# The input norm of a hybrid decoder layer: weight spread over partitions in PSUM, factor and weight in one pass, buffers on the other side of SBUF, products of the identity first

## The chip, the cores and the metric

The kernel runs on one core of a Trainium2 chip. The metric is the device time of one execution in microseconds. Three runs of the kernel before gave 758.95, 758.96 and 759.19 us, median 758.96 us. Engines are named as the profile names them: PE (TensorE), DVE (VectorE), ACT (ScalarE), POOL (GpSimd), SP (the queue that issues most DMAs).

## The reference, cut to what matters

The program is one decoder layer on 512 tokens of width 1024. The change touches only its first step, the RMS norm that feeds the input projection:

```
def _rmsnorm(x, g):
    xf = x.astype(jnp.float32)
    y = xf * lax.rsqrt(jnp.mean(xf * xf, axis=-1, keepdims=True) + NORM_EPS)
    return y.astype(x.dtype) * g
...
    h = _rmsnorm(x, norm_g[i])
    proj = h @ w_in[i]
```

Everything after it (three token mixers, merge, output projection, per-layer embedding, final norm) is unchanged.

## The kernel before, in words

Products run on PE from split operands: a value v is kept as a high part (`hH`, `wh`) and a low part v - high (`hL`, `wl`), and each product is three: high x high, low x high, high x low (`mm` on line 61, called in `fm_block`). `h` is needed transposed, with its 1024 channels on the partitions in 8 blocks of 128 and the 512 tokens along the free side: `hH` and `hL`, 128 x 8 x 512.

The start of the program makes them (lines 198 to 226). x comes in as four tiles of 128 tokens (`xs_`). For each tile t, ACT squares it with a running sum (L213), DVE scales the sum (L214), POOL takes the power -1/2 (L215), which is the row factor `rsx`, and DVE multiplies the tile by it (L216). Then, for each half a of 512 channels, PE transposes four 128 x 128 blocks into PSUM (`xt_ps`, L221), DVE multiplies by the norm weight, which stands one value per partition by then (`ngp`, L223), ACT rounds the result to the high part (L224), and DVE or POOL subtracts for the low part (L225; table `XL`). The buffers of this stage (`xp`: `xs_`, `sqj`, `tg`) lie on SBUF's left side and are given back at `xp_ctx.close()`; the pools opened after it take their place, `cpp` among them, which holds `kc2`, `w1t` and `w2t`.

The first consumer is the block of the compression inputs (lines 249 to 264, "kc" below): for two halves of 256 tokens and two projections kv, 24 products each of 256 columns, 96 in all. It needs four loads of `w_in` (`wr`), rounded by ACT (`wh`, L77) and subtracted by DVE (`wl`, L78; the table `KL` names the engine). Each load covers four of the eight channel blocks, 12 products in each half. ACT copies the PSUM results into `kc2` (L263, L264); two PSUM buffers alternate (`pmm`). After it come the blocks of `rs_block`, 24 products of 512 columns each.

POOL makes the constants of the whole kernel before anything else (masks, indicators: lines 96 to 132, and `prow`, `hm`). Parameters come in as rows of `prow` (14 small DMAs on SP), and PE transposes them (`par_ps`, L268).

Each engine works off its instructions in order. The order is set by a scheduler at build time from its own estimates; the program can pin it (`tc.issue_after(x)` puts a block behind instruction x on x's engine, `tc.keep_in_program_order` keeps the order as written).

Of the kernel before, what the change touches and what calls it, by code (L numbers as in the profile page):

```python
# [17 lines left out]
NEG = -1e30  # L18
WE, NR, NH, NL = 560, 4, 5, 5
NG = 6  # L20
XL = "GV"
XB = 4
XP = 3
KL = "V"
KCA = 3
BS = 3
BO = 1
# [12 lines left out]
def f(ap):  # L40
    return ap.bitcast(F32)
# [3 lines left out]
def hybrid_kernel(ctx, tc, x, p, norm_g, w_in, cmp_w1, cmp_w2, cmp_pe, sg_ln_g, sg_ln_b, sg_w, sg_b,  # L45
# [49 lines left out]
    identb = const.tile([128, 128], BF, name="identb")
    V.tensor_copy(identb, ident)
    trib = const.tile([128, 128], BF, name="trib")
    G.memset(trib, 0.0)
    G.affine_select(out=trib, in_=trib, pattern=[[-1, 128]], compare_op=OP.is_ge, fill=NEG, base=0,
                    channel_multiplier=1)  # L100
    cmask = const.tile([128, 4, 32], BF, name="cmask")
    G.memset(cmask, 0.0)
    G.affine_select(out=cmask, in_=cmask, pattern=[[128, 4], [-16, 32]], compare_op=OP.is_ge, fill=NEG,
                    base=-31, channel_multiplier=1)
    rowm = const.tile([128, 1], F32, name="rowm")
    G.memset(rowm, 1.0)
    G.affine_select(out=rowm, in_=rowm, pattern=[[0, 1]], compare_op=OP.is_ge, fill=0.0, base=-31,
                    channel_multiplier=1)
    gmask = const.tile([128, 2, 64], BF, name="gmask")
    G.memset(gmask, 1.0)  # L110
    for r in (0, 64):
        for ar in range(2):
            G.affine_select(out=gmask[r:r + 64, ar, :], in_=gmask[r:r + 64, ar, :], pattern=[[1, 64]],
                            compare_op=OP.is_ge, fill=0.0, base=ar - 1, channel_multiplier=-1)
    smask = const.tile([128, 8, 64], BF, name="smask")
    G.memset(smask, 1.0)
    G.memset(smask[:, :, 0:1], 0.0)
    tri = const.tile([128, 128], BF, name="tri")
    G.memset(tri, 1.0)
    G.affine_select(out=tri, in_=tri, pattern=[[1, 128]], compare_op=OP.is_ge, fill=0.0, base=0,  # L120
                    channel_multiplier=-1)
    mhalf = const.tile([128, 32], F32, name="mhalf")
    G.memset(mhalf, -0.5)
    bones = const.tile([128, 128], BF, name="bones")
    G.memset(bones, 0.0)
    G.memset(bones[0:64, 0:64], 1.0)
    G.memset(bones[64:128, 64:128], 1.0)
    hind = const.tile([128, 4, 8], F32, name="hind")
    G.memset(hind, 0.0)
    for q in range(4):  # L130
        for e in range(2):
            G.memset(hind[e * 64:e * 64 + 64, q, 2 * q + e:2 * q + e + 1], 1.0)

    ng8 = const.tile([8, 128], F32, name="ng8")
    ngp = const.tile([128, 8], F32, name="ngp")
# [10 lines left out]
    hH = hp.tile([128, 8, 512], R, name="hH")  # L146
    hL = hp.tile([128, 8, 512], R, name="hL")
# [56 lines left out]
    dr = {}  # L204
    for nm, w in (("su", 512), ("sv", 512), ("sz", 512), ("rz", 512), ("nz", 512), ("y1", 512), ("sg", 512)):
        dr[nm] = tc.dram_tile([NG * 128 if nm == "sg" else 512, w], F32, name="dr_" + nm)
    ng_ps = xps.tile([128, 8], F32, tag="par", name="ng_ps", bufs=1)
    PE.transpose(ng_ps, ng8, ident[0:8, 0:8])
    V.tensor_copy(ngp, ng_ps)
    for t in range(4):  # L210
        ts = slice(t * 128, (t + 1) * 128)
        sqj = xp.tile([128, 1024], F32, tag="sqj", name="sqj", bufs=2)
        S.activation(sqj, xs_[:, t, :], AF.Square, accum_out=ssx[:, t:t + 1])  # L213
        V.tensor_scalar(rsx[:, t:t + 1], ssx[:, t:t + 1], 1.0 / 1024, 1e-6, op0=OP.mult, op1=OP.add)  # L214
        G.tensor_tensor(rsx[:, t:t + 1], rsx[:, t:t + 1], mhalf[:, 0:1], OP.pow)  # L215
# [90 lines left out]
    for kv in range(2):  # L306
# [10 lines left out]
        else:  # L317
            V.tensor_copy(sl, slp.rearrange("p (g n) -> p g n", g=2).unsqueeze(2).to_broadcast([128, 2, 4, 32]))
            for g in range(2):
# [4 lines left out]
                                       op0=OP.mult, op1=OP.subtract)  # L324
# [39 lines left out]
    for i, src in ((0, rk_w2), (1, rk_a2)):  # L364
        a, o = (slice(0, 64), slice(64, 128)) if i == 0 else (slice(64, 128), slice(0, 64))
# [39 lines left out]
    for q in range(4):  # L405
        rs_block(q)
        rs_block(8 + q)
        ps = rps.tile([128, 4, 128], F32, tag="y0", name="v_ps")
# [64 lines left out]
        for c0 in (0, 4):  # L473
            ps = rps.tile([128, 4, 128], F32, tag="y1", name="bk_ps")
# [63 lines left out]
    for c in range(8):  # L538
# [40 lines left out]
        if u == 1:  # L579
            t = c // 2  # L580
            ts = slice(t * 128, (t + 1) * 128)
# [16 lines left out]
            ps = rps.tile([128, 2, 2, 2, 64], F32, tag="g", name="yt_ps")  # L598
# [75 lines left out]
    for g in range(8):  # L674
# [3 lines left out]
                               op0=OP.add, op1=OP.mult)  # L678
# [318 lines left out]
```

## Time and profile before

| | |
|---|---|
| median of three runs | 758.96 us |
| profiled execution, its own time | 758.88 us |
| its span | 757.1 us |
| PE busy | 720.5 us (95%) |
| DVE, ACT, POOL busy | 403.1, 353.7, 327.6 us |
| first product of the kc block that uses `wl` | 17.44 us |
| first product of the block after it (512 columns) | 31.13 us |

Times in rows count from the span's start; 1.78 us of the execution's own time lie outside it. PE works through the program almost without a gap, so what counts for the change is at what time PE leaves the kc block.

### The profile page before, as it was taken

How to read it: one execution, taken by the hardware profiler on the slowest of the kernel's cores; microseconds unless marked ns; L12 is line 12 of the kernel's file. 1: busy time of each engine (PE TensorE's matmuls, PEld its weight loads, DVE VectorE, ACT ScalarE, POOL GpSimd, SP SyncE). 2: the span in 40 equal slices, each digit the busy share in tenths (PEclk: the TensorE clock that was granted, in tenths of full speed). 3: DMA queues.
4: the chain of work that ended last, by engine and by line, in shares of the span. 5: the costliest groups of instructions: out<-in, count | busy, mean ns of one | idle time of the engine just before them, and what ended most of it. 6: DMA issues, size and time to landing. Idle time of an engine off the chain costs nothing.

```text
span 757.1 us, 13075 instructions
## 1 busy us (share of the span) xinstructions
PE 720.5 (95%) x4941; PEld 610.3 (81%) x4941; DVE 403.1 (53%) x747; ACT 353.7 (47%) x743; POOL 327.6 (43%) x304
## 2 busy tenths in 40 slices
PE   4999999999996999999899999989999999999995
PEld 4888788899875987778777777867877888998995
DVE  6531688658817553456558456387655222216335
ACT  6454565533351332334464655476654333127453
POOL 6455731020335343424534335533445656256563
PEclk9999999999998999999999999999999999999999
DMA  5853222234553353346434222211117433222222
GB/s 197 186 142 85 64 73 59 72 97 118 147 171 111 100 165 112 103 140 182 138 84 125 57 56 56 71 29 42 43 47 250 121 98 110 72 98 75 79 70 112
DMA packets 106689, 78.73 MB, mean 104 GB/s; under 512 B 5569, under 2 KB 97282, under 8 KB 106626
## 3 DMA queue, kind: packets, MB, share of 16 engines
q1 hardware_dynamic: 105890, 75.27, 34.6%
q10 hardware_dynamic: 736, 2.63, 0.8%
q8 instruction: 39, 0.64, 0.3%
q14 instruction: 24, 0.20, 0.1%
HBM read 67.91 MB, written 9.96 MB: 103 GB/s over the span
## 4 chain that ended last, share of the span: by engine, by line
PE 83%; DVE 6%; DMA 3%; ACT 3%; issue 2%; POOL 1%; SPq 0%; ACTq 0%; POOLq 0%; DVEq 0%
PE mm_ps L61 66%; PE s_ps L61 3%; PE o_ps L61 2%; PE g_ps L61 2%; PE p_ps L861 2%; PE Yp L61 1%; DMA vn<-dr_sv 1%; DMA lnb<-in_sg_ln_b_dram 1%; PE r_ps L61 1%; DVE mx L847 1%; PE mx_ps L61 1%; DVE vn L671 1%; DVE pl L865 1%; ACT wh L77 1%; DMA zs<-dr_y 1%
## 5 line engine op out<-in xcount | busy, mean ns | idle before, releaser
L78 POOL TENSOR_TENSOR wl<-wr,wh 128x512 fp32r<-128x512 f32 (+1 forms) x168 | 225.0, 1348 | 292.8 <-ACT wh L77 279.1
L77 ACT CAST wh<-wr 128x512 fp32r<-128x512 f32 (+1 forms) x194 | 119.1, 620 | 162.7 <-PE mm_ps L61 112.3
L61 PE MATMUL mm_ps<-hH,wh 128*128 128x512 f32 (+1 forms) x440 | 174.9, 397 | 5.7 <-ACT gate L747 2.8
L61 PE MATMUL mm_ps<-hL,wh 128*128 128x512 f32 (+1 forms) x440 | 172.9, 393 | 0.0
L61 PE MATMUL mm_ps<-hH,wl 128*128 128x512 f32 (+1 forms) x440 | 172.2, 392 | 0.0
L61 PEld LDWEIGHTS mm_ps<-hH,wh 128*128 128x128 f32 x440 | 83.9, 191 | 24.0 <-ACT gate L747 3.5
L61 PEld LDWEIGHTS mm_ps<-hH,wl 128*128 128x128 f32 x440 | 83.8, 191 | 17.9 <-DVE wl L78 0.3
L61 PEld LDWEIGHTS mm_ps<-hL,wh 128*128 128x128 f32 x440 | 84.0, 191 | 16.7 <-issue 0.2
L61 PE MATMUL mm_ps<-wh,hL 128*128 128x256 f32 (+1 forms) x224 | 65.3, 292 | 0.0
L61 PE MATMUL mm_ps<-wl,hH 128*128 128x256 f32 (+1 forms) x224 | 64.7, 289 | 0.0
L61 PE MATMUL mm_ps<-wh,hH 128*128 128x256 f32 (+1 forms) x224 | 64.3, 289 | 0.0
L61 PEld LDWEIGHTS mm_ps<-wh,hH 128*128 128x128 f32 x224 | 42.8, 192 | 1.3 <-issue 0.5
L61 PEld LDWEIGHTS mm_ps<-wh,hL 128*128 128x128 f32 x224 | 43.0, 192 | 0.9 <-issue 0.5
L61 PEld LDWEIGHTS mm_ps<-wl,hH 128*128 128x128 f32 x224 | 42.9, 191 | 0.8
L865 DVE TENSOR_TENSOR pl<-p_ps,ph 128x512 fp32r<-128x512 f32 x40 | 27.1, 684 | 26.8 <-ACT ph L864 26.7
L61 PE MATMUL mm_ps<-ysH,wh 128*128 128x512 f32 x96 | 38.6, 402 | 0.2 <-ACT ysH L716 0.2
L61 PE MATMUL mm_ps<-ysL,wh 128*128 128x512 f32 x96 | 38.4, 400 | 0.2 <-DVE ysL L717 0.2
L61 PE MATMUL mm_ps<-ysH,wl 128*128 128x512 f32 x96 | 38.2, 398 | 0.0
L848 ACT ACTIVATE P<-s_ps,mx 128x512 f32<-128x512 f32 (+3 forms) x64 | 33.4, 532 | 7.8 <-DVE mx L847 5.5
L61 PE MATMUL mm_ps<-wh,mH 128*128 128x256 f32 x128 | 36.1, 286 | 0.6 <-DVE x L910 0.6
L61 PE MATMUL mm_ps<-wl,hT 128*128 128x256 f32 x128 | 35.8, 281 | 0.0
L61 PE MATMUL mm_ps<-wl,mH 128*128 128x256 f32 x128 | 35.8, 281 | 0.0
(336 smaller groups left out, 1437.1 us busy)
## 6 DMA issues: line engine op xcount, KB each, us to landing
wr<-in_w_in_dram SPq DMA_DIRECT2D x130, 256.0 KB
wr<-in_w_branch_dram SPq DMA_DIRECT2D x24, 256.0 KB
wr<-in_w_o_dram SPq DMA_DIRECT2D x16, 256.0 KB
wr<-in_w_ple_gate_dram SPq DMA_DIRECT2D x16, 256.0 KB
xs__129<-in_x_dram SPq DMA_DIRECT2D x4, 512.0 KB
w1t<-in_cmp_w_dram SPq DMA_DIRECT2D x4, 512.0 KB
x<-in_x_dram ACTq DMA_DIRECT2D x4, 512.0 KB
out_dram<-x SPq DMA_DIRECT2D x8, 256.0 KB
```

Of the source, the lines that this page charges most:

```text
L61: return PE.matmul(o, a, b, start=start, stop=stop, **kw).ins
L77: S.copy(h[:, :m], raw[:, :m])
L78: ph_["l"].tensor_tensor(l[:, :m], raw[:, :m], f(h[:, :m]), OP.subtract)
L671: V.tensor_scalar(vn[:, t, :], vn[:, t, :], mv[:, t, 0:1], rs4[:, t:t + 1], op0=OP.subtract, op1=OP.mult)
L847: V.tensor_reduce(mx[:, hh:hh + 1], s_ps[:, :W], axis=AX.X, op=OP.max, negate=True)
L848: S.activation(P[:, hh, :W], s_ps[:, :W], AF.Exp, bias=mx[:, hh:hh + 1], accum_out=sm[:, hh:hh + 1])
L861: PE.transpose(p_ps[:, hh * 128:hh * 128 + 128], P[:, hh, kt * 128:kt * 128 + 128], ident)
L865: V.tensor_tensor(pl, p_ps, f(ph), OP.subtract)
```

## The change

The norm weight is loaded as one row of 1024 (`ngr`) and spread over all partitions by two products with a column of ones, into two PSUM banks (`ngb`). DVE then applies row factor and weight at once to each half tile, before the transposes (`scalar_tensor_tensor`), so that the product with `ngp` after them (L223) goes, and ACT and DVE take high and low part straight from PSUM. The order of DVE's instructions is written out. 14 products of the identity with itself stand at the head of PE's program (`wu`). `XP` (PSUM buffers of the transposes) goes from 3 to 4. The four `wl` of the kc block, and all four low parts `hL` of POOL, change engine: `wl` to POOL (`KL`), `hL` to DVE. All constants but `ident`, `mhalf`, `one` and the zeros of `kc2` are made behind the fourth power on POOL (`issue_after(pws[3])`). The pools `xp` and `pw` lie on SBUF's right side.

```
-XL = "GV"
-XB = 4
-XP = 3
-KL = "V"
+XP = 4
+WU = 14
+KL = "G"
...
-    xp = xp_ctx.enter_context(tc.tile_pool(name="xp", bufs=1))
+    xp = xp_ctx.enter_context(tc.tile_pool(name="xp", bufs=1, side="right"))
...
-    S.dma_start(ng8, norm_g[0].rearrange("(a b) -> a b", b=128))
+    ngr = xp.tile([1, 1024], F32, name="ngr")
+    one = xp.tile([1, 128], F32, name="one")
+    S.dma_start(ngr, norm_g)
+    G.memset(one, 1.0)
...
-    ng_ps = xps.tile([128, 8], F32, tag="par", name="ng_ps", bufs=1)
-    PE.transpose(ng_ps, ng8, ident[0:8, 0:8])
-    V.tensor_copy(ngp, ng_ps)
+    wu = pmm.tile([128, 512], F32, tag="mm", name="wu")
+    for _ in range(WU):
+        mm(wu[:, 0:128], ident, ident, True, True)
+    ngb = xps.tile([128, 2, 512], F32, tag="ngb", name="ngb", bufs=1)
+    for a in range(2):
+        mm(ngb[:, a, :], one, ngr[:, a * 512:a * 512 + 512], True, True)
+    pin = tc.keep_in_program_order
...
-        V.tensor_scalar(xs_[:, t, :], xs_[:, t, :], rsx[:, t:t + 1], None, op0=OP.mult)
...
-            tg = xp.tile([128, 4, 128], F32, tag="tg", name="tg", bufs=XB)
-            V.tensor_tensor(tg, ps, ngp[:, 4 * a:4 * a + 4].unsqueeze(2).to_broadcast([128, 4, 128]), OP.mult)
-            hcp.append(S.copy(hH[:, ks, ts], tg).ins)
-            (V if XL[a] == "V" else G).tensor_tensor(hL[:, ks, ts], tg, f(hH[:, ks, ts]), OP.subtract)
+    def x_fac(t):
+        r = rsx[:, t:t + 1]
+        pin(V.tensor_scalar(r, ssx[:, t:t + 1], 1.0 / 1024, 1e-6, op0=OP.mult, op1=OP.add))
+        pws.append(G.tensor_tensor(r, r, mhalf[:, 0:1], OP.pow).ins)
+
+    def x_turn(t):
+        ts = slice(t * 128, (t + 1) * 128)
+        for a in range(2):
+            xa = xs_[:, t, a * 512:a * 512 + 512]
+            pin(V.scalar_tensor_tensor(xa, xa, rsx[:, t:t + 1], ngb[:, a, :], op0=OP.mult, op1=OP.mult))
+            ps = xps.tile([128, 4, 128], F32, tag="xt", name="xt_ps")
+            for k in range(4):
+                PE.transpose(ps[:, k, :], xa[:, k * 128:k * 128 + 128], ident)
+            hcp.append(S.copy(hH[:, 4 * a:4 * a + 4, ts], ps).ins)
+            xts[t, a] = ps
+
+    def x_low(t):
+        ts = slice(t * 128, (t + 1) * 128)
+        for a in range(2):
+            h = slice(4 * a, 4 * a + 4)
+            pin(V.tensor_tensor(hL[:, h, ts], xts[t, a], f(hH[:, h, ts]), OP.subtract))
+
+    for fn, t in ((x_fac, 0), (x_turn, 0), (x_fac, 1), (x_fac, 2), (x_turn, 1), (x_fac, 3), (x_low, 0), (x_turn, 2),
+                  (x_low, 1), (x_turn, 3), (x_low, 2), (x_low, 3)):
+        fn(t)
     xp_ctx.close()
+
+    with tc.issue_after(pws[3]):
+        identb = const.tile([128, 128], BF, name="identb")
+        V.tensor_copy(identb, ident)
+        trib = const.tile([128, 128], BF, name="trib")
...
+        G.memset(prow, 0.0)
```

On POOL, at the end of the constants and the start of the kc block, the program before stands so (`rsx` is the power, `hL` a low part, `wl` the first weight's low part that is not DVE's):

```order
L132 MEMSET hind 64x1 x8
L242 MEMSET hm 32x1 x4
L215 TENSOR_TENSOR rsx<-rsx,mhalf 128x1 x3
L225 TENSOR_TENSOR hL<-tg,hH 128x4x128
L215 TENSOR_TENSOR rsx<-rsx,mhalf 128x1
L225 TENSOR_TENSOR hL<-tg,hH 128x4x128 x3
L78 TENSOR_TENSOR wl<-wr,wh 128x512
```

And now (line numbers are those of the changed file), with the constants between the powers and the weights:

```order
masks.py:199 AFFINE_SELECT ident<-ident 128x128
L185 TENSOR_TENSOR rsx<-rsx,mhalf 128x1 x4
L214 MEMSET trib 128x128
L218 MEMSET cmask 128x128
...
L241 MEMSET bones 64x64
L246 MEMSET hind 64x1 x8
L264 MEMSET hm 32x1 x4
L77 TENSOR_TENSOR wl<-wr,wh 128x512 x5
```

The constants moved from the head of POOL's program to between the fourth power and the first `wl`, and the four `wl` of the kc block joined the queue behind them.

PE's program starts so before (`ng_ps` is the turned weight, `xt_ps` the transposes of x, `mm_ps` the kc block):

```order
L208 MATMUL ng_ps<-ident,ng_115 128x8
L221 MATMUL xt_ps<-ident,xs__129 128x128 x24
L61 MATMUL mm_ps<-hH,wh 128x256
L61 MATMUL mm_ps<-hL,wh 128x256
L221 MATMUL xt_ps<-ident,xs__129 128x128 x8
L61 MATMUL mm_ps<-hH,wh 128x256
L61 MATMUL mm_ps<-hL,wh 128x256
L61 MATMUL mm_ps<-hH,wl 128x256
```

And now:

```order
L60 MATMUL wu<-ident 128x128 x14
L60 MATMUL ngb<-ngr,one 128x512 x2
L194 MATMUL xt_ps<-ident,xs__89 128x128 x20
L60 MATMUL mm_ps<-hH,wh 128x256
L194 MATMUL xt_ps<-ident,xs__89 128x128 x4
L60 MATMUL mm_ps<-hL,wh 128x256
L60 MATMUL mm_ps<-hH,wh 128x256
L60 MATMUL mm_ps<-hL,wh 128x256
L194 MATMUL xt_ps<-ident,xs__89 128x128 x8
L60 MATMUL mm_ps<-hH,wl 128x256
```

16 products stand ahead of the first transpose; as before, four of the 96 products of the kc block precede the first one with `wl`, and all transposes do.

On SP, the DMA queue, the program before goes (`prow` are the 14 small parameter loads, cut here; `w1t` and `w2t` the compression weights):

```order
L181 DMA xs__129<-in_x_dram 128x1024 x4
L75 DMA wr<-in_w_in_dram 128x4x128 x4
L266 DMA prow<-in_rk_mu_dram 13x128
...
L75 DMA wr<-in_w_in_dram 128x4x128 x4
L285 DMA w2t<-in_cmp_w_dram 128x64 x4
L290 DMA w1t<-in_cmp_w_dram 64x16x128 x4
```

And now:

```order
L146 DMA xs__89<-in_x_dram 128x1024 x4
L74 DMA wr<-in_w_in_dram 128x4x128 x4
L307 DMA w2t<-in_cmp_w_dram 128x64 x4
L312 DMA w1t<-in_cmp_w_dram 64x16x128 x4
L288 DMA prow<-in_rk_mu_dram 13x128
...
L74 DMA wr<-in_w_in_dram 128x4x128 x4
```

The compression weights (2 MB) moved ahead of the parameters and of the second four weights. In the rest of the program PE's order differs only in a few places of the stage behind the `rs_block`s.

## Rows read from the trace of the kernel before

**Rows 1.** The page's head: span; busy us, share, instructions of each engine.
```profile
span 757.1 us, 13075 instructions
...
PE 720.5 (95%) x4941; PEld 610.3 (81%) x4941; DVE 403.1 (53%) x747; ACT 353.7 (47%) x743; POOL 327.6 (43%) x304
```

**Rows 2.** Waits of PE, 0 to 70 us: waiter, releaser, total, times, longest.
```profile
PE xt_ps L221 <- DVE rsx L214: 5.8, 1, 5.8
...
PE mm_ps L61 <- ACT wh L77: 1.7, 1, 1.7
PE mm_ps L61 <- ACT kc L264: 1.2, 1, 1.2
```

**Rows 3.** Timeline of PE, 24 to 60 us: start, duration, idle before.
```profile
25.33 0.39 PE L61 MATMUL mm_ps<-hH,wh 128*128 128x256 f32 x1 [1.21 <-ACT kc L264]
...
31.13 0.39 PE L61 MATMUL mm_ps<-hH,wh 128*128 128x512 f32 x1
```

**Rows 4.** Timeline of ACT, 20 to 40 us: the first copy.
```profile
23.80 0.37 ACT L263 COPY kc<-mm_ps 64x256 f32<-64x256 f32 x1 [2.11 <-DVE hL L225]
```

**Rows 5.** Timeline of all engines, PE's way into the kc block.
```profile
8.37 5.14 PE L221 MATMUL xt_ps<-ident,xs__129 128*128 128x128 f32 x24 [5.82 <-DVE rsx L214]
...
15.22 0.39 PE L61 MATMUL mm_ps<-hH,wh 128*128 128x256 f32 x1 [1.71 <-ACT wh L77]
...
15.73 1.25 PE L221 MATMUL xt_ps<-ident,xs__129 128*128 128x128 f32 x8
...
16.71 1.28 DVE L78 TENSOR_TENSOR wl<-wr,wh 128x512 fp32r<-128x512 f32 x2
...
17.44 0.58 PE L61 MATMUL mm_ps<-hH,wl 128*128 128x256 f32 x1
```

**Rows 6.** Windows of 2 us: busy time by engine, then PE's granted clock.
```profile
16.00:18.00 2.00, 1.97 (x12) 1.67 (x11) 2.00 (x5) 1.77 (x4) 0.67 (x1) 0.62 0.58 188
18.00:20.00 2.00, 2.00 (x12) 2.00 (x11) 2.00 (x3) 0.62 (x1) 1.81 (x2) 0.53 0.84 235
20.00:22.00 2.00, 2.00 (x19) 2.00 (x19) 2.00 (x3) 1.14 (x2) 1.57 (x2) 1.00 0.87 229
```

**Rows 7.** Timeline of POOL: ident, and the constants' first and last.
```profile
0.93 0.20 POOL L98 MEMSET trib<- 128x128 bf16 x1
...
1.31 0.29 POOL masks.py:199 TENSOR_SCALAR_AFFINE_SELECT ident<-ident 128x128 f32<-128x128 f32 x1
...
6.38 0.49 POOL L242 MEMSET hm<- 32x1 f32 x4
```

**Rows 8.** Timeline of PE, 91 to 93 us: one f32 product of 512 columns.
```profile
91.58 1.02 PE L61 MATMUL bo<-m,bor 128*128 128x512 f32 x2
```

**Rows 9.** Line 221 from 13 to 14 us: durations in ns, min/median/max.
```profile
L221 PE MATMUL xt_ps<-ident,xs__129 x4: 273/300/421, 12.7 to 13.2; 128*128 128x128 f32 x4
```

**Rows 10.** Groups of DVE by form, 0 to 60 us: busy, mean ns, idle.
```profile
L341 DVE SCALAR_TENSOR_TENSOR AR<-mm_ps,omu,Sb 128x512 f32<-128x512 f32 x3 | 2.2, 747 | 9.6 <-ACT Sb L339 9.6
```

**Rows 11.** Timeline of all engines, the factor's round trip over POOL.
```profile
5.62 0.15 DVE L214 TENSOR_SCALAR rsx<-ssx 128x1 f32<-128x1 f32 x1 [2.86 <-ACT sqj L213]
...
8.23 0.15 DVE L214 TENSOR_SCALAR rsx<-ssx 128x1 f32<-128x1 f32 x1
...
8.45 0.56 POOL L215 TENSOR_TENSOR rsx<-rsx,mhalf 128x1 f32<-128x1 f32 x1 [0.93 <-DVE rsx L214]
...
9.04 0.75 DVE L216 TENSOR_SCALAR xs__129<-xs__129,rsx 128x1024 f32<-128x1024 f32 x1 [0.67 <-POOL rsx L215]
...
9.15 1.06 ACT L213 ACTIVATE sqj<-xs__129 128x1024 f32<-128x1024 f32 x1 [0.21 <-DMA xs__129<-in_x_dram]
```

**Rows 12.** The tile wr, 0 to 60 us: POOL's low parts, ns min/median/max.
```profile
L78 POOL TENSOR_TENSOR wl<-wr,wh x13: 1284/1297/2450, 21.2 to 59.0; 128x512 fp32r<-128x512 f32 x13
```

**Rows 13.** Timeline of SP, 20 to 60 us: issue of the compression weights.
```profile
26.04 5.24 SPq L290 DMA_DIRECT2D w1t<-in_cmp_w_dram  x4
```

**Rows 14.** Windows of 2 us while w1t lands: last column GB/s.
```profile
29.00:31.00 2.00, 2.00 (x19) 2.00 (x18) 0.37 (x1) 1.92 (x5) 1.29 (x1) 1.00 1.04 227
```

More of the change, by code (lines that the diff above doesn't have):

```diff
@@ L94, in hybrid_kernel @@
     make_identity(nc, ident)
[L95 to L121, printed above, removed]
     mhalf = const.tile([128, 32], F32, name="mhalf")
     G.memset(mhalf, -0.5)
[L124 to L135, printed above, removed]
     par = const.tile([128, 128], F32, name="par")
@@ L172, in hybrid_kernel @@
     hcp = []
+    pw_ctx = ExitStack()
+    pw = pw_ctx.enter_context(tc.tile_pool(name="pw", bufs=1, side="right"))
     xp_ctx = ExitStack()
-    xp = xp_ctx.enter_context(tc.tile_pool(name="xp", bufs=1))
+    xp = xp_ctx.enter_context(tc.tile_pool(name="xp", bufs=1, side="right"))
     xps = xp_ctx.enter_context(tc.tile_pool(name="xps", bufs=XP, space=PSUM))
@@ L210, in hybrid_kernel @@
+    pin = tc.keep_in_program_order
+    pws, xts = [], {}
     for t in range(4):
-        ts = slice(t * 128, (t + 1) * 128)
         sqj = xp.tile([128, 1024], F32, tag="sqj", name="sqj", bufs=2)
         S.activation(sqj, xs_[:, t, :], AF.Square, accum_out=ssx[:, t:t + 1])
-        V.tensor_scalar(rsx[:, t:t + 1], ssx[:, t:t + 1], 1.0 / 1024, 1e-6, op0=OP.mult, op1=OP.add)
-        G.tensor_tensor(rsx[:, t:t + 1], rsx[:, t:t + 1], mhalf[:, 0:1], OP.pow)
-        V.tensor_scalar(xs_[:, t, :], xs_[:, t, :], rsx[:, t:t + 1], None, op0=OP.mult)
+    def x_fac(t):
+        r = rsx[:, t:t + 1]
+        pin(V.tensor_scalar(r, ssx[:, t:t + 1], 1.0 / 1024, 1e-6, op0=OP.mult, op1=OP.add))
+        pws.append(G.tensor_tensor(r, r, mhalf[:, 0:1], OP.pow).ins)
@@ L217, in hybrid_kernel @@
+    def x_turn(t):
+        ts = slice(t * 128, (t + 1) * 128)
         for a in range(2):
-            ks = slice(4 * a, 4 * a + 4)
+            xa = xs_[:, t, a * 512:a * 512 + 512]
+            pin(V.scalar_tensor_tensor(xa, xa, rsx[:, t:t + 1], ngb[:, a, :], op0=OP.mult, op1=OP.mult))
             ps = xps.tile([128, 4, 128], F32, tag="xt", name="xt_ps")
             for k in range(4):
-                PE.transpose(ps[:, k, :], xs_[:, t, (4 * a + k) * 128:(4 * a + k + 1) * 128], ident)
-            tg = xp.tile([128, 4, 128], F32, tag="tg", name="tg", bufs=XB)
@@ new lines, in hybrid_kernel @@
+    for fn, t in ((x_fac, 0), (x_turn, 0), (x_fac, 1), (x_fac, 2), (x_turn, 1), (x_fac, 3), (x_low, 0), (x_turn, 2),
+                  (x_low, 1), (x_turn, 3), (x_low, 2), (x_low, 3)):
+        fn(t)
+    xp_ctx.close()
+    with tc.issue_after(pws[3]):
+        identb = const.tile([128, 128], BF, name="identb")
+        V.tensor_copy(identb, ident)
+        trib = const.tile([128, 128], BF, name="trib")
+        G.memset(trib, 0.0)
+        G.affine_select(out=trib, in_=trib, pattern=[[-1, 128]], compare_op=OP.is_ge, fill=NEG, base=0,
+                        channel_multiplier=1)
+        cmask = const.tile([128, 4, 32], BF, name="cmask")
+        G.memset(cmask, 0.0)
+        G.affine_select(out=cmask, in_=cmask, pattern=[[128, 4], [-16, 32]], compare_op=OP.is_ge, fill=NEG,
+                        base=-31, channel_multiplier=1)
+        rowm = const.tile([128, 1], F32, name="rowm")
+        G.memset(rowm, 1.0)
+        G.affine_select(out=rowm, in_=rowm, pattern=[[0, 1]], compare_op=OP.is_ge, fill=0.0, base=-31,
+                        channel_multiplier=1)
+        gmask = const.tile([128, 2, 64], BF, name="gmask")
+        G.memset(gmask, 1.0)
+        for r in (0, 64):
+            for ar in range(2):
+                G.affine_select(out=gmask[r:r + 64, ar, :], in_=gmask[r:r + 64, ar, :], pattern=[[1, 64]],
+                                compare_op=OP.is_ge, fill=0.0, base=ar - 1, channel_multiplier=-1)
+        smask = const.tile([128, 8, 64], BF, name="smask")
+        G.memset(smask, 1.0)
+        G.memset(smask[:, :, 0:1], 0.0)
+        tri = const.tile([128, 128], BF, name="tri")
+        G.memset(tri, 1.0)
+        G.affine_select(out=tri, in_=tri, pattern=[[1, 128]], compare_op=OP.is_ge, fill=0.0, base=0,
+                        channel_multiplier=-1)
+        bones = const.tile([128, 128], BF, name="bones")
+        G.memset(bones, 0.0)
+        G.memset(bones[0:64, 0:64], 1.0)
+        G.memset(bones[64:128, 64:128], 1.0)
+        hind = const.tile([128, 4, 8], F32, name="hind")
+        G.memset(hind, 0.0)
+        for q in range(4):
+            for e in range(2):
+                G.memset(hind[e * 64:e * 64 + 64, q, 2 * q + e:2 * q + e + 1], 1.0)
+        G.memset(prow, 0.0)
@@ L239, in hybrid_kernel @@
     hm = const.tile([128, 4], F32, name="hm")
-    G.memset(hm, 0.0)
-    for hh in range(4):
-        G.memset(hm[32 * hh:32 * hh + 32, hh:hh + 1], 1.0)
+    with tc.issue_after(pws[3]):
+        G.memset(hm, 0.0)
+        for hh in range(4):
+            G.memset(hm[32 * hh:32 * hh + 32, hh:hh + 1], 1.0)
     cp_ctx = ExitStack()
```

3 lines of the change are left out of this document (removed).

## The prediction

> **What bounds the kernel now.** I read the page's first part for the span and the shares, then who makes PE wait in the first 70 us, then the stretch to 31 us engine by engine. PE is busy 95% of the time [rows 1], so the change is worth what it does to the moment at which PE leaves the kc block for the products of 512 columns: 31.13 us [rows 3]. Before that moment PE has three waits: for the first row factor, for the first rounded weight, and for ACT's copies out of PSUM [rows 2]. After it that list, which runs to 70 us, holds none.
>
> The start reads like this. The transposes begin at 8.37 us; four products of the kc block are through before the last transposes; the first product that needs `wl` starts at 17.44 us, right behind DVE's first `wl` [rows 5]. From there 92 of the 96 products are left. At the clock's higher level (2.4 GHz) the 48 of the second half take 31.13 - 25.33 = 5.80 us, 0.121 each [rows 3], so 92 and the parameter transpose take 11.24 us. The granted clock is 0.62 in 16 to 18 us and 0.53 in 18 to 20, then 1.00 [rows 6]: so half of full speed for (0.38 + 0.47) x 2 / 0.5 = 3.4 us, of which 2.4 lie behind 17.44, a loss of 1.2 us. And 1.21 us are lost where the second half waits for the copies, which had waited for DVE's last `hL` because `kc2` lies in the memory of `tg` [rows 3, 4]. 17.44 + 11.24 + 1.2 + 1.21 = 31.09, against 31.13 in the trace. So three things can move the end: when the first `wl` is ready, PE's clock then, and the copies' wait.
>
> **The first wl.** In the changed order it stands on POOL behind the constants, these behind the fourth power, that behind the fourth scaled sum on DVE, that behind four combined products on DVE, and these behind the spread weight in PSUM. The wait of the first combined product covers both halves of the spread weight, as its semaphore counts the second. Step by step:
>
> 1. `ident` is ready at 1.31 + 0.29 = 1.60 us [rows 7]; PE starts at 1.65.
> 2. An f32 product is two records on PE where a transpose is one. A transpose at the lower level (1.2 GHz) is 5.14 / 24 = 0.214 us [rows 5]; so an identity product is 0.43 at the lower level and 0.21 at the higher. Fourteen are 6.0 or 3.0 us. In the trace the transposes got short (421 to 273 ns) at some 12.8 us, 4.4 us after PE began [rows 5, 9]. Taken from 1.65 that is 6.05: ten at the lower level, four at the higher, end 6.85.
> 3. A 512-column f32 product at the higher level is four times the 128-column one, 0.85 us; its two records show as 1.02 [rows 8], so 0.17 is the tail of the last. Two end at 8.55, with the tail and a semaphore 8.8.
> 4. Two combined products on DVE: the nearest row, the same form with one operand in PSUM, is 0.747 [rows 10], and neighbours overlap by some 0.07: 1.42, so 10.2. The squares are not the limit: the first sum is scaled at 5.62, the fourth square ends at 10.2 [rows 11].
> 5. Scaled sum, power on POOL, next product: 8.23 to 9.04, 0.81 [rows 11]: 11.0. Two more products: 12.45.
> 6. Fourth scaled sum and power: 8.23 to 8.45 + 0.56, 0.78 [rows 11]: 13.2.
> 7. The constants: they ran from 0.93 to 6.38 + 0.49 = 6.87 [rows 7], less 0.3 for `ident` and `mhalf`, which stay in front: 5.65. Now 18.9. In the program before this stretch was hidden, since POOL stood at the head of no chain then.
> 8. One `wl` on POOL is 1.30 [rows 12]: 20.2; PE goes on at 20.3.
>
> That is 2.9 us later than 17.44. The combined products, `hL` and transposes of tiles 2 and 3 end by some 18.5 (four more DVE pairs of 1.4 behind 12.6) and are covered. The other three `wl` follow at 1.30 each, while PE takes 12 x 0.121 = 1.45 for each load: covered, with little to spare.
>
> **The copies' wait.** `xp` no longer lies where `kc2` does, so the copies wait for PE alone. Four copies (1.5 us) fit beside the 24 products of the other buffer (2.9 us). Gain 1.21 us, all on the path.
>
> **The clock.** PE is well fed until 8.7 us, then has 32 transposes and four products, some 4 us of work at the higher level, spread over 11.6 us. In the trace before, the pause from 13.5 to 15.2 with little work around it was enough for the clock to fall at 16.5 [rows 5, 6]. I take it as low when the stream starts, and the stretch to last as in rows 6: up to 3.4 us, a loss of up to 1.7, less what was gone by before the stream. I take 1.5, against 1.2 before: 0.3 us lost. Bounds: none lost (gain 1.2) and 3.4 (two such stretches).
>
> The Trainium skill, page TensorE: Matmul & The Clock Gate, section Part 4: PE-mode transpose, says that transposes don't count as PE work for the clock. This trace disagrees: 24 transposes and nothing else preceded the rise of rows 9. By the page the clock is low at 20.3 for certain; by the trace the transposes count, and a rival below keeps it high.
>
> **Loads.** `w1t` (2 MB) now goes ahead of the 14 parameter loads and the second four weights. It needed 5.24 us of issue [rows 13] and lands at 227 GB/s [rows 14], some 9 us: about 10.5 to 20 us. The parameters then arrive at some 24.7; PE's transpose of them stands 44 products behind the first `wl`, at about 27. The second four weights are issued from some 22.7 and needed from 33. Cost nothing, with 2 us of cover. The 8 products with `ngp`, 4 scalings and 4 `hL` of POOL that go lie beside the chain above, so they are worth nothing.
>
> **Sum.** +2.9 (first `wl`) - 1.2 (copies) + 0.3 (clock) = +1.9 us. The profiled execution took 758.88 us, 0.08 below the median: forecast 760.8 us. PE's waits behind 60 us hang on chains that the change does not touch; I let them move with the rest, with half a microsecond of doubt. A measurement of this kernel can tell 0.2%, 1.5 us, from no change, so 757.4 and 760.5 are the borders.
>
> **Rivals.**
>
> *The clock is high when the stream starts.* PE is warmed earlier and the transposes hold it. Then the loss is 0 in place of 1.2 before: +2.9 - 1.2 - 1.2 = +0.5, 759.3 us. For it: the transposes count, and they come in eight groups without a pause of 1.7 us until 18.5. Against it: the pause from 18.5 to 20.3, and only a third of the time is work.
>
> *Faster: the clock is high from the first identity products.* Then they end at 4.65, the spread weight at 6.4, and the squares are the limit: third sum at 9.1 (the fourth square starts then [rows 11]), second pair of products to 10.55, fourth power 11.3, constants 17.0, first `wl` 18.3, PE 18.4. +1.0 - 1.2 - 1.2 = -1.4, 757.4 us. It decides if the products run at 0.21 from the start. Against it: the transposes at 8.37 started at the lower level.
>
> *Much slower: the clock rises only behind the spread weight.* All 14 at 0.43 end at 7.65, the spread weight at 1.71 each at 11.1; every later step moves by 2.5 us: PE at 22.8, +4.4 in all, 763.3 us. It decides if PE's records are still long when the spread weight comes. A rise in between gives 761.5 to 762.5.
>
> *The parameters come late.* If `w1t` takes 3 us more than the 9 worked out, the parameter transpose, in order in PE's program, stops the stream for about 1 us: 762 us. For it: 14 small loads wait behind 2 MB. Against it: 2 us of cover.
>
> **How the numbers follow.** Forecast 45%, its own range 760.0 to 761.6; clock held 25%; faster 10%; much slower 12%; parameters late 8%. The range of 8 in 10 runs from 758.6, below the second case, to 763.0, leaving out the fast case and the end of the slow one. Slower by over 0.2%: 34 of the forecast's 45 points, and 20 of the slow ones: 54%. Within: 11 points of the forecast, 25 of the held clock, 2 of the fast one: 38%. Faster: 8%.
>
> **What would show it.** In the changed profile: the 14 products, some at 0.43 and some at 0.21 us, and the spread weight's second half ending near 8.7; the first combined product near 8.8; four powers on POOL, the last near 13.2, then 5.6 us of constants, then four `wl`; the first product with `wl` near 20.3, released by POOL; granted clock about one half behind it for some 3 us; no wait for the copies; the first 512-column product near 33.0. It is wrong if PE goes on before 18.5, if POOL is done with its constants before the weights are rounded, or if PE leaves the kc block before 31.1.

## The result, and the profile after

The changed kernel takes 763.02 us (median of seven runs) against 758.95 us of the kernel before beside it: a ratio of 1.0058, interval 1.0043 to 1.0073. It is slower, as forecast, but by 4.07 us and not by 1.9. The profiled execution took 763.6 us, its span is 761.9, 4.8 more than in [rows 1].

PE's waits from 0 to 70 us in the changed kernel (waiter, releaser, total, times, longest), for [rows 2]:

```profile
PE wu L60 <- POOL ident masks.py:199: 1.8, 1, 1.8
PE mm_ps L60 <- POOL wl L77: 1.7, 1, 1.7
PE par_ps L290 <- DMA prow<-in_cmp_pe_dram: 1.1, 1, 1.1
PE xt_ps L194 <- DVE xs__89 L191: 1.1, 2, 0.9
...
PE mm_ps L60 <- ACT kc L286: 0.8, 1, 0.8
```

The waits for `wl` and `par_ps` are new; the one for the copies of `kc` is still there. The timeline of PE (start, duration, idle before) puts them in their places, for [rows 3, 5]:

```profile
1.82 5.97 PE L60 MATMUL wu<-ident 128*128 128x128 f32 x28 [1.82 <-POOL ident masks.py:199]
7.71 1.98 PE L60 MATMUL ngb<-ngr,one 1*128 1x512 f32 x4
...
20.91 0.58 PE L60 MATMUL mm_ps<-hH,wl 128*128 128x256 f32 x1 [1.70 <-POOL wl L77]
...
28.99 0.30 PE L290 MATMUL par_ps<-ident,prow 128*128 128x128 f32 x1 [1.11 <-DMA prow<-in_cmp_pe_dram]
...
32.97 0.39 PE L60 MATMUL mm_ps<-hH,wh 128*128 128x256 f32 x1 [0.79 <-ACT kc L286]
...
35.90 0.39 PE L60 MATMUL mm_ps<-hH,wh 128*128 128x512 f32 x1
```

PE leaves the kc block at 35.90 instead of 31.13 us: 4.77 later, which is the whole growth of the span. The first product with `wl` makes 3.47 of it (20.91 - 17.44), the parameters 1.11, the copies 0.79 - 1.21 = -0.42, and the clock some 0.5. These make 4.66.

That the 4.77 us reappear as 4.8 at the end is in part luck. Read at the first record of a tile, PE is 4.5 us behind the kernel before at `ss_ps` (75 us), 6.0 at `iv_ps` (212), 7.2 at `ut_ps` (336) and 5.0 at `x_ps` (658).

The chain in front of `wl`, in the timelines of DVE and of POOL:

```profile
9.80 1.41 DVE L191 SCALAR_TENSOR_TENSOR xs__89<-xs__89,rsx,ngb 128x512 f32<-128x512 f32 x2 [3.89 <-PE ngb L60]
```
```profile
13.49 0.55 POOL L185 TENSOR_TENSOR rsx<-rsx,mhalf 128x1 f32<-128x1 f32 x1 [1.07 <-DVE rsx L184]
...
18.98 0.49 POOL L264 MEMSET hm<- 32x1 f32 x4
19.56 5.02 POOL L77 TENSOR_TENSOR wl<-wr,wh 128x512 fp32r<-128x512 f32 x4
```

It runs as the prediction has it, but late: by 1.0 us at the first combined product, by 0.6 at the first product with `wl`. What the prediction did not have is in SP's timeline, for [rows 13], and in SP's waits:

```profile
10.45 5.74 SPq L312 DMA_DIRECT2D w1t<-in_cmp_w_dram  x4
16.30 2.59 SPq L288 DMA_DIRECT2D prow<-in_rk_mu_dram  x1
...
22.26 0.25 SPq L288 DMA_DIRECT2D prow<-in_rk_lnx_g_dram  x1
24.77 0.25 SPq L288 DMA_DIRECT2D prow<-in_rk_lnx_b_dram  x1
...
25.77 1.70 SPq L288 DMA_DIRECT2D prow<-in_cmp_pe_dram  x4
27.57 2.05 SPq L74 DMA_DIRECT2D wr<-in_w_in_dram  x4
```
```profile
SPq L288 <- DMA w1t<-in_cmp_w_dram: 3.9, 2, 2.2
```

The parameter loads stop twice, for some 2 us each, before 22.26 and 24.77, and both times SP waits for `w1t`: by the windows below its traffic ends at about 24 us. The second four weights are issued at 27.57, not at 22.7. In ACT's program the cast of the first of them stands ahead of twelve of the sixteen copies of `kc` (timeline of ACT; the fifth copy is shown), for [rows 4]:

```profile
30.80 0.62 ACT L76 CAST wh<-wr 128x512 fp32r<-128x512 f32 x1 [4.00 <-DMA wr<-in_w_in_dram]
31.45 0.36 ACT L285 COPY kc<-mm_ps 64x256 f32<-64x256 f32 x1
```

ACT idles 4 us in front of that cast, with finished products waiting in PSUM behind it. So the old wait for the copies went and another came, with another cause.

Windows of 2 us (busy times by engine, then PE's granted clock, DMA share, GB/s), for [rows 6]:

```profile
12.00:14.00 2.00, 1.80 (x9) 1.40 (x8) 2.00 (x5) 1.01 (x3) 0.93 (x3) 0.50 1.02 195
14.00:16.00 2.00, 1.10 (x9) 0.81 (x7) 2.00 (x5) 1.98 (x4) 2.00 (x14) 0.98 1.24 187
16.00:18.00 2.00, 1.32 (x9) 0.99 (x9) 2.00 (x4) 2.00 (x5) 1.73 (x11) 1.00 1.24 181
...
20.00:22.00 2.00, 1.09 (x5) 1.09 (x6) 1.75 (x4) 0.00 (x0) 2.00 (x2) 0.73 1.23 189
22.00:24.00 2.00, 2.00 (x11) 2.00 (x11) 0.00 (x0) 0.00 (x0) 2.00 (x3) 0.50 0.92 133
24.00:26.00 2.00, 2.00 (x18) 2.00 (x17) 0.00 (x0) 0.67 (x2) 0.58 (x1) 0.92 0.01 2
```

The clock is at its lower level behind 20.9 us, as forecast: (0.27 + 0.50 + 0.08) x 2 = 1.7 us lost. The last column shows the loads at 181 to 189 GB/s (181 to 192 in all windows from 14 to 22), where 227 GB/s [rows 14] was reckoned.

### The profile page after: what moved, and what is told of

The parts are those of the page before. It is cut to its first block, busy times and chain, and to the rows that moved or that the text cites. A ratio compares the mean times of both kernels' runs of the same rounds, so it can differ in the third digit from the quotient of the medians.

```text
span 761.9 us, 13127 instructions
## 1 busy us (share of the span) xinstructions
PE 728.1 (96%) x4972; PEld 616.0 (81%) x4972; DVE 399.2 (52%) x742; ACT 353.2 (46%) x743; POOL 327.1 (43%) x305
## 4 chain that ended last, share of the span: by engine, by line
PE 82%; DVE 6%; DMA 5%; ACT 3%; issue 2%; POOL 1%; SPq 0%; ACTq 0%; POOLq 0%; DVEq 0%
PE mm_ps L60 64%; PE s_ps L60 3%; PE o_ps L60 2%; PE g_ps L60 2%; PE p_ps L883 2%; DMA prow<-in_rk_mu_dram 1%; PE Yp L60 1%; DMA vn<-dr_sv 1%; DMA lnb<-in_sg_ln_b_dram 1%; DMA zs<-dr_nz 1%; PE r_ps L60 1%; PE wu L60 1%; DVE mx L869 1%; PE mx_ps L60 1%; DVE vn L693 1%
## 5 line engine op out<-in xcount | busy, mean ns | idle before, releaser
L77 POOL TENSOR_TENSOR wl<-wr,wh 128x512 fp32r<-128x512 f32 (+1 forms) x172 | 231.1, 1353 | 294.1 <-ACT wh L76 280.8
```

Of the source, the lines that this page charges most:

```text
L77: ph_["l"].tensor_tensor(l[:, :m], raw[:, :m], f(h[:, :m]), OP.subtract)
```

## The experiments

The first theory had two losses that add up, a late `wl` and late loads, where the parameters and the cast are one wait each; its rivals were that the loads cost nothing and that the clock makes the loss. In diffs "c" stands for the lines of constants.

**Parameters ahead of `w1t`** (prow0): zeroing `prow` early lets its loads be issued first.

```
-        G.memset(prow, 0.0)          # last line of c, behind the fourth power
     prow = pw.tile([128, 128], F32, name="prow")
+    G.memset(prow, 0.0)
```

> One line moved: prow is zeroed at the head of POOL's program again and not among the late constants, so the 14 parameter loads stand ahead of w1t in SP's queue as before the change. Theory (two separate losses: a late first wl and late loads): the first product with wl stays at 20.9 us, the parameter transpose no longer waits (1.11 us gone) and the copies of kc no longer stand behind a late cast (0.79 us gone); the first 512-column product at 34.0 us instead of 35.90, the time 761.1 us. Rival (the loads cost nothing, all of the loss is the late wl and the clock): 35.9 us and 763.0 us, with PE's wait at 28 us put down to something else.

Measured: 772.59 us, 1.0192 (1.016 to 1.0224). Both theory and rival fell: the parameters' wait went, but the time is some 10 us above the changed kernel's. SP, ACT and PE in the timelines of this run:

```profile
16.71 5.20 SPq L312 DMA_DIRECT2D w1t<-in_cmp_w_dram  x4
22.01 2.67 SPq L74 DMA_DIRECT2D wr<-in_w_in_dram  x1
```
```profile
33.19 0.62 ACT L76 CAST wh<-wr 128x512 fp32r<-128x512 f32 x1 [13.66 <-DMA wr<-in_w_in_dram]
```
```profile
35.23 0.58 PE L60 MATMUL mm_ps<-hH,wh 128*128 128x256 f32 x1 [7.70 <-ACT kc L286]
```

A weight issued right behind `w1t` is cast 11 us later, and as all copies of `kc` stand behind that cast here, PE waits 7.7 us. Behind that wait the granted clock is 0.50 until about 41 us, which costs nearly 3 us more. This points at whether `w1t` (2 MB) stands ahead of the second four weights; the run late below tests it.

**Constants first, loads as changed** (const):

```
+    <c, without prow>                # in front of mhalf, at the head of POOL's program
+    with tc.issue_after(pws[3]):
+        G.memset(prow, 0.0)
```

> The constants go back to the head of POOL's program, all but the zeroing of prow, which stays behind the fourth power; so SP's order stays that of the changed kernel (w1t ahead of the parameters and of the second four weights). Theory: wl follows the powers at once, PE goes on with wl at 17 us (20.9 in the changed kernel), but then waits some 5 us for the parameters until 29.0 us and for the cast behind the second weights; the first 512-column product stays at 35.5 to 36.2 us and the time at 763.0 us. Rival (the late wl is the whole loss): 32 us and 759.2 us. Rival (the clock): the long pause at 23 to 29 us makes it fall once more, 37 us and 764 us.

Measured: 766.33 us, 1.0114 (1.009 to 1.0139). The first product with `wl` moved from 20.91 to 17.33 us, and nothing was gained: PE stands at the parameters and at the copies (timeline of PE).

```profile
29.90 0.45 PE L287 MATMUL par_ps<-ident,prow 128*128 128x128 f32 x1 [5.26 <-DMA prow<-in_cmp_pe_dram]
...
33.73 0.58 PE L60 MATMUL mm_ps<-hH,wh 128*128 128x256 f32 x1 [3.38 <-ACT kc L283]
```

The theory had this right for the parameters, and missed that an order dealt anew puts all copies behind the cast. The block is left at 40.85: the clock fell in the long pause, as the last rival had it, and is at 0.50 from 28 to 36 us, which costs the products behind the waits some 1.8 us.

**Constants and parameters first** (first): both edits above.

```
+    <c>                              # in front of mhalf
+    G.memset(prow, 0.0)              # behind the tile prow
```

> All constants and the zeroing of prow back at the head of POOL's program: both losses undone together; the identity products, the spread weight, the combined products and the memory side stay. Theory: PE goes on with wl at 17 us, no wait for parameters or copies, the first 512-column product at 29.8 to 30.5 us (31.13 in the kernel before, which paid 1.21 us for the copies), the time 757.3 to 758.0 us. Rival (the identity products and the spread weight cost by themselves): 32 us or more, 759.5 us or more. Rival (the w1t loads still ahead of the second weights hold PE at the first 512-column product): 31 to 33 us.

Measured: 772.05 us, 1.0189 (1.0158 to 1.0221); the kc block left at 43.55, with 11.1 us of wait for the copies (PE's waits):

```profile
PE mm_ps L60 <- ACT kc L282: 11.1, 1, 11.1
```

The expected gain of 5 us was a loss of 9. The run has two sources of delay less and is the second slowest of all: again `w1t` stands right in front of the second weights.

**No identity products** (wu0):

```
-WU = 14
+WU = 0
```

> The 14 identity products are left out, all else as in the changed kernel (SP's order too). Theory: the spread weight is done at 5.3 us instead of 9.7, the squares are the limit as in the kernel before (fourth power some 3 us earlier, at 11 us), the constants end at 16.6 us, PE goes on with wl at 18.0 us instead of 20.9; the zeroing of prow comes 3 us earlier too, but w1t still stands ahead of the parameters, so PE waits for them until 28.5 to 29 us and the first 512-column product stays at 35.5 to 36 us: 762.7 to 763.0 us. Rival (the late wl is the whole loss): 33 us, 760.1 us. Rival (the products pay by a higher clock): slower than the changed kernel, 764 us.

Measured: 764.97 us, 1.0088 (1.006 to 1.0116). PE's timeline shows `wl` 2.4 us earlier and the same end of the parameters' wait as in the changed kernel:

```profile
18.52 0.39 PE L60 MATMUL mm_ps<-hH,wl 128*128 128x256 f32 x1 [1.34 <-POOL wl L77]
...
29.01 0.44 PE L290 MATMUL par_ps<-ident,prow 128*128 128x128 f32 x1 [5.01 <-DMA prow<-in_cmp_pe_dram]
```

An earlier `wl` is worth nothing while the loads bind. The time is near the last rival's 764 us, but its interval overlaps that of the changed kernel: no gain or loss by the 14 products is told apart here.

**`w1t` behind the second weights** (late): nothing but the order on SP.

```
+    for i in w1d:                    # the loads of w2t and w1t
+        tc.add_manual_dep(i, wdm[7].name, <order only>)   # wdm[7]: last of the second four
```

> Only the order of loads is undone: the four loads of w1t (and w2t) are issued behind the second four weights, as in the kernel before; constants, identity products and the memory side stay as changed. What the runs before this one point to: the load of the second four weights is served late because w1t stands ahead of it, ACT casts that weight ahead of its copies of kc, and PE waits for the copies. Theory: the first product with wl stays at 20.9 us, no wait for parameters (they are there by 25 to 26, needed at 27.8), none for the copies, the first 512-column product at 34.0 us (35.90 in the changed kernel), 761.1 us. Rival (order of loads beside the point): 35.9 us, 763.0 us. Rival (w1t now too late for the product hid that reads it): kc block left at 34.0 but a new wait of 2 us or more behind 36 us.

Measured: 765.05 us, 1.0061 (1.0041 to 1.0081). The block is left at 33.82 as forecast (34.0), without a wait for parameters or copies. The time did not fall. Where it went (timelines of PE and ACT):

```profile
41.53 3.68 PE L60 MATMUL hid<-w1t,blk 128*64 128x128 f32 x62 [0.27 <-DMA w1t<-in_cmp_w_dram]
52.26 0.33 PE L329 MATMUL slp<-ident,th 128*128 128x128 f32 x1 [1.74 <-DVE th L327]
```
```profile
42.13 0.62 ACT L77 CAST wh<-wr 128x512 fp32r<-128x512 f32 x1 [6.60 <-DMA wr<-in_w_in_dram]
...
50.83 0.26 ACT L326 ACTIVATE th<-hid 128x128 f32<-128x128 f32 x1
```
`hid` ends at 45.2, but `th` stands on ACT behind casts of the third group of weights, whose loads now come behind `w1t`. PE waits 2.0 us at `hid` and `slp`, close to the last rival, and that takes the 2.08 us back: at the first `ss_ps` (75 us) PE stands where the changed kernel has it, to 0.1 us, and still at the first `iv_ps` (212). From there the two profiles drift apart, to -1.4 us at 335 and +1.5 at the end. A stretch of low clock around 370 us is part of that, but a stretch near 248 us is shorter by as much, and over all windows behind 40 us both lose the same to the clock (5.1 us). Why the span ends 1.5 us longer stays open; the two ratios, 1.0061 and 1.0058, don't differ beyond their intervals.

**The same with the constants first** (late_first), **and without the products** (late_first_wu0): late, with the edits of first, and of wu0.

> The constants at the head of POOL's program and w1t issued behind the second four weights; identity products, spread weight, combined products and the memory side stay. Theory (two losses that add up): PE goes on with wl at 16.9 us, as with the constants first alone, but the 11.1 us wait for the copies of kc is gone; the first 512-column product at 30.0 to 30.8 us (31.13 before the change), 757.3 to 758.1 us. Rival (the spread weight and the identity products cost by themselves): 31.5 us or more, 759.4 us or more. Rival (the low clock of the start lasts longer since PE starts its stream at 17): 31.5 us with granted clock under 0.6 for 3.4 us behind 17.

> As the constants first with w1t late, and without the 14 identity products. Theory (the products only delay the spread weight): spread weight done at 6.9 us instead of 9.1, fourth power at 11.6, first wl on POOL from 13.4, PE goes on with wl at 14.8 us, the first 512-column product at 28.0 to 29.0 us, 755.4 to 756.4 us: faster than both kernels. Rival (the second weights bind: their load waits for wl and for the parameter loads, issued from 15 to 17 us): 30 us, 757.3 us. Rival (the products paid for themselves by the clock): no earlier than with them, 30.5 us.

Measured: 759.92 us, 1.0009 (0.9994 to 1.0024), and 759.97 us, 1.0004 (0.9989 to 1.0019). The blocks are left at 29.28 and 28.86 us, 1.9 and 2.3 before the kernel before, and the time is its own. Both were expected faster. PE's waits in late_first show the taker again:

```profile
PE slp L325 <- DVE th L323: 1.9, 1, 1.9
...
PE hid L60 <- DMA w1t<-in_cmp_w_dram: 1.1, 1, 1.1
```

**The memory side undone, constants first** (left_first): the tile pool `xp` without `side="right"`, with the edits of first.

```
-    xp = xp_ctx.enter_context(tc.tile_pool(name="xp", bufs=1, side="right"))
+    xp = xp_ctx.enter_context(tc.tile_pool(name="xp", bufs=1))
```

> Constants at the head of POOL's program and the buffers of the norm back on the side where kc and w1t lie; identity products and the rest stay. The memory then holds w1t back until the norm is done, and SP's program has the second four weights ahead of it without being told so. Theory (the free memory let w1t pass the second weights, and that is what cost 11 us with the constants first): no long wait for the copies of kc; PE goes on with wl at 17 us, a wait of up to 1.2 us for the copies, the first 512-column product at 29.3 to 30.5 us, 759 to 761 us against 772.05 with the buffers on the other side. Rival (the place in memory has nothing to do with it): 43 us and 772 us.

Measured: 760.13 us, 1.0018 (1.0004 to 1.0032), 12 us less than first, with the block left at 31.61. SP's timeline has the weights in front without being told:

```profile
18.70 6.52 SPq L74 DMA_DIRECT2D wr<-in_w_in_dram  x5
...
27.23 5.04 SPq L308 DMA_DIRECT2D w1t<-in_cmp_w_dram  x4
```

So the wait for memory that the change removed had kept 2 MB of loads out of the way of 1 MB that was needed sooner.

**Identity products in the kernel before** (before_wu, 14; before_wu12, 12):

```
+    wu = pmm.tile([128, 512], F32, tag="mm", name="wu")
+    for _ in range(WU):
+        mm(wu[:, 0:128], ident, ident, True, True)
```

> The kernel before, with the 14 products of the identity put at the head of PE's program and nothing else changed. Theory: PE has nothing to do there until 8.37 us, so the products (1.65 to 7.6 us) delay nothing; the transposes start at the higher level, but the pause behind them lets the clock fall again: first 512-column product at 31.0 to 31.3 us, 758.9 us, the same. Rival (they keep the clock up through the kc block's start): the loss of 1.2 us goes, 29.9 us, 757.7 us.

> The kernel before with 12 products of the identity at the head of PE's program instead of 14. With 12 the scheduler leaves the order of the rest of the program as it was before (it differs in 5 rows of PE and 8 of DVE), with 14 it deals the order anew far into the program. Theory (the gain of the run with 14 came from the new order in the middle, where PE's waits at 230 to 300 us fell from 6.5 to 4.5 us and one stretch of low clock went, not from the products): the waits for SV at 240 us stay at 3.2 and 3.3 us, 759.0 to 759.8 us, the same as before. Rival (the products themselves pay): 756.5 to 757.2 us.

Measured: 756.85 us, 0.9973 (0.9958 to 0.9987), and 759.05 us, 1.0002 (0.9988 to 1.0017). Neither leaves the block sooner than 31.13 us (31.93 and 33.35), so the products don't pay there. What the 14 gain lies behind the block. The theory named the waits of the middle; these are, from 70 to 340 us, with 14 and with 12:

```profile
PE mm_ps L62 <- DVE st L640: 3.3, 1, 3.3
PE r_ps L62 <- DVE rs L672: 1.2, 1, 1.2
```
```profile
PE r_ps L62 <- DVE SV L576: 4.5, 1, 4.5
PE st_ps L62 <- DVE SV L561: 0.7, 1, 0.7
```

With 12, in the old order, they are 5.2 us where the kernel before has 6.5 and where 6.5 was expected; so the waits alone don't carry the theory. The order does show in the profiles. The transposes `ws_ps` (line 656 of the kernel before) stand in two places, and the stretch from PE's first `iv_ps` to its first `ut_ps`, some 1300 records of the same work, goes with them:

| order of the middle | profiles | first `ws_ps` | `iv_ps` to `ut_ps` |
|---|---|---|---|
| `ws_ps` behind the first `yt_ps` | before, before_wu12, after, late and the seven other runs above | 264 to 277 us | 120.9 to 123.9 us |
| `ws_ps` ahead of it | before_wu and the five runs below with `slp` moved | 239 to 245 us | 118.1 to 120.0 us |

So the new order goes with some 3.5 us less in that stretch (medians 122.3 and 118.8), and the 0.27% may be that; no run changes this order alone, so it is not shown as the cause.

**`slp` later on PE** (lfw_slp and lf_slp: late_first_wu0 and late_first with it):

```
+    tc.add_manual_dep(slpt, mms[nmm + 65].name, <order only>)   # mms: all products as written; slp 15 later
```

> As the constants first, w1t late and no identity products, and besides the transpose slp moved 15 products of 512 columns later in PE's program. Theory (what the kc block gained there, 2.3 us against the kernel before, was given back at slp, where PE waits 2.2 us for th, which stands on ACT behind casts of weights whose loads come behind w1t): the wait for th is gone, the kc block ends at 28.9 us as before the move, 757.3 to 758.0 us, faster than both kernels. Rival (the order dealt anew in the middle decides): PE's waits at 190 to 300 us change by 1 us or more from 6.8 and the time is anywhere from 756.5 to 761.

> As the run before it with the 14 identity products left in. Theory: kc block left at 29.3 us, slp without a wait, a wait of 1 us for w1t at hid; 758.0 to 758.6 us, half a microsecond more than without the products. Rival (the products are worth their time in the clock): 757 us or less, faster than without them.

Measured: 751.42 us, 0.9889 (0.9869 to 0.9908), and 752.75 us, 0.9913 (0.9894 to 0.9931): faster than both kernels, by more than the wait at `slp`. That is gone in both; the wait at `hid` is 2.0 and 1.6 us. The rest came behind it: at the first `iv_ps` lf_slp is 3.8 us ahead of late_first, and the stretch from there to `ut_ps`, now in the other order of the middle, takes another 3.1 us less. The two differ by 0.24%, with intervals that overlap: whether the products cost anything there is not told apart.

**Loads against `wl` on equal ground** (after_slp, late_slp, before_slp: the changed kernel, late, and the kernel before, each with `slp` moved):

> The changed kernel with nothing but the transpose slp moved 15 products of 512 columns later on PE. In the middle its order is that of the run with constants first, w1t late and slp moved (span 750.9 us with the kc block left at 28.98 and a wait of 1.6 us at hid). Theory (the kc block's end counts one for one): kc block left at 35.9 us, 6.9 later, no wait at hid as w1t came early: 750.9 + 6.9 - 1.6 = 756.2 us of span, 758 us. Rival (the move of slp gives only the wait that stood there, none in the changed kernel): 762.5 to 763.5 us.

> The changed kernel with w1t behind the second four weights and slp moved. Theory: kc block left at 33.8 us, 2.1 us before the run above, some 0.3 us of wait at hid: a span of 750.9 + 4.8 - 1.3 = 754.4 us, 1.8 us below the run above: the loads' place costs about 2 us, and against the run with the constants first as well (752.75 us) the late wl costs 3.5 us. Rival (the loads' place costs nothing in the end, as the run with w1t late by itself had it): the same as the run above to 0.5 us.

> The kernel before, with nothing but slp moved 15 products later on PE. Theory (the move deals the middle of the program anew, and that is worth some 5 us in any of these kernels): kc block left at 31.1 us, a span of some 750.9 + 2.1 - 1.6 = 751.4 to 754 us, 752 to 755 us. Rival (in the kernel before PE doesn't wait at slp, so the move brings nothing): 758.5 to 759.5 us.

Measured: after_slp 757.90 us, 0.9997 (0.9986 to 1.0009); late_slp 755.62 us, 0.9970 (0.9957 to 0.9982); before_slp 756.28 us, 0.9982 (0.9970 to 0.9993). PE's timelines, of after_slp and of late_slp:

```profile
29.29 0.45 PE L293 MATMUL par_ps<-ident,prow 128*128 128x128 f32 x1 [4.00 <-DMA prow<-in_cmp_pe_dram]
...
36.39 0.40 PE L62 MATMUL mm_ps<-hH,wh 128*128 128x512 f32 x1
```
```profile
31.61 0.40 PE L62 MATMUL mm_ps<-hH,wh 128*128 128x512 f32 x1
```

The loads' place costs 0.27%, 2.0 us, as expected (1.8), and these intervals don't touch. The two profiles lie 4.8 us apart at the block's end: the parameters' wait is 4.00 us in after_slp, as PE comes to it sooner while it ends as late as in the changed kernel (29.29 against 28.99), and the clock falls behind it (0.50 from 30 to 32 us), while in late_slp the clock is high through the block. A wait of 2.3 us at `hid` then takes back a part, and from 75 to 229 us PE is 2.5 us ahead. The constants' place costs 0.57% more (late_slp to lf_slp), 4.3 us by the ratios and 2.9 by the medians, of runs on different occasions; in the profiles PE is 3.5 us ahead from 72 to 212 us, where 3.5 were expected. Moving `slp` alone brought 0.2% to the kernel before, less than the theory's 3 to 7 us, and 0.6% to the changed one, though PE waits at `slp` in neither; in both it came with the other order of the middle. Why more in one than in the other stays open. So the change itself costs less on this ground: 757.90 against 756.28 us, with intervals that overlap, though the block is left 5.3 us later.

| run | first product with `wl` | kc block left | waits at hid and slp | span | median |
|---|---|---|---|---|---|
| before | 17.44 | 31.13 | none | 757.1 | 758.95 |
| after | 20.91 | 35.90 | none | 761.9 | 763.02 |
| first | 17.36 | 43.55 | none | 770.3 | 772.05 |
| late | 21.19 | 33.82 | 2.0 | 763.4 | 765.05 |
| late_first | 17.34 | 29.28 | 3.0 | 757.9 | 759.92 |
| before_slp | 17.44 | 31.13 | none | 754.4 | 756.28 |
| after_slp | 19.82 | 36.39 | none | 757.0 | 757.90 |
| late_slp | 20.47 | 31.61 | 2.3 | 753.6 | 755.62 |
| lf_slp | 17.01 | 28.98 | 1.6 | 750.9 | 752.75 |
| lfw_slp | 15.31 | 27.81 | 2.0 | 750.7 | 751.42 |

## Why the prediction was wrong in size

The sign and the chain in front of `wl` held: the constants took 5.5 us (5.65 forecast), POOL released PE, and the clock was low for 3.4 us behind it. That the end of the kc block counts one for one held between these two profiles, in part by luck; with `slp` moved, 5.3 us at the block's end (before_slp, after_slp) were 2.6 us of span. The time lies next to the 763.3 us of the rival "much slower", but not by its road: of its 2.5 us only 0.6 came. Of the 2.9 us between 33.0 and 35.90, the steps below make 2.7.

**The step that failed is "Loads", which "cost nothing, with 2 us of cover".** It cost 1.9 us: 1.11 for the parameters and 0.79 for the copies. It went wrong three times. `w1t` was given 9 us at 227 GB/s, from 10.5 to 20; it came at 181 to 192 GB/s until about 24. The parameter loads were taken to flow behind it, but SP stopped twice among them, 3.9 us in all, to wait for it. And the second weights were called "needed from 33", by PE's first product with them; ACT needed the first one before the copies of `kc`, and PE needs those copies from 32.2 (32.97 - 0.79). The rival of late parameters named the first wait and its 1 us, with 8%, and no case had the cast. The run late shows the step itself: with `w1t` behind the second weights both waits are gone. That the loads count in the time, 2.0 us, is shown by after_slp against late_slp, both with `slp` moved.

**The first `wl`**: 20.91 instead of 20.3 (0.6 us). All 14 identity products ran at the lower level (5.97 us in all, 0.43 each), where ten and four were forecast, and the first combined product started at 9.80, not 8.8; 0.4 of that second was won back behind. The sum gave the 14 products 5.2 us; over the runs with them they took 4.87 to 6.25, so this term alone moves by up to 1.4 us from run to run. The rival "much slower" had the cause, but not that the spread weight would run at the higher level (1.98 us).

**The copies' wait**: its old cause went as forecast, 1.21; 0.79 came back from the cast. **The clock**: 1.7 us lost, 1.5 forecast. The rival with a high clock did not happen here, but it did in late_slp, where the clock was at 0.5 from 10 to 20 us and back at 1.00 when the stream began: there the block was left 2.2 us before late's.

From 10.6 to 14.4 us PE of the changed kernel ran 16 transposes and nothing else, and the granted clock went from 0.50 (12 to 14 us) to 0.98 (14 to 16). The Trainium skill, TensorE: Matmul & The Clock Gate, Part 4: PE-mode transpose, says that transposes don't count as PE work for the clock; this rise is against it. But in late_slp the same 16 transposes ran alone from 10.2 to 14.3 us, and the clock stayed at 0.50 until 20. What decided between the two is not shown.

**Behind 60 us** "half a microsecond of doubt" was allowed. In the changed kernel it came out even, but on the way the distance to the kernel before went from 4.5 to over 7 us, and the move of one transpose was worth 0.2 to 1.2% over five kernels, waits at `slp` included, so the doubt was too small.

## What to carry to other kernels

A wait for memory can be what keeps a large load behind a small urgent one. Before such a wait is removed, read what the queue's order becomes, and then, for each load that falls behind, which instruction in which engine's program reads it first and what stands behind that instruction: here a cast on ACT ahead of copies that PE needed.

Two delays on parallel paths hide each other: undoing either alone gained nothing or lost (const, late), and only with the next join behind them (`slp`) out of the way did the profiles show what each is worth.

An edit at the program's start can deal the order anew hundreds of microseconds behind it. Before two times are compared, look whether both have the same order there: here two orders of one stretch went with a difference of some 3.5 us, nearly the size of the effect in question.

## What the runs showed of the hardware that was not expected

In prow0 a weight of 256 KB, issued at 22.01 us right behind the 2 MB of `w1t`, was cast at 33.19, 11 us later; in the changed kernel, issued at 27.57 when `w1t` had landed, it was cast 3.2 us later.

The granted clock of a window does not show the lower level at PE's start: in late_first_wu0 the window from 4 to 6 us has 1.00, while the four records of the spread weight took 3.78 us, 0.94 each, against 1.98 us in the changed kernel. The level there is read from durations.
